# A two-group encoder layer in split precision: two sets of plane buffers in branch b, the factor of x moved into the gates, other PSUM banks for two sums

## The chip, the cores and the metric

The kernel runs on one core of a Trainium2 chip. The metric is the device time of one launch in microseconds (us). Three runs of the kernel before gave 1679.86, 1680.59 and 1681.42; their median is 1680.59 us.

## The reference, cut to what matters

One layer of an encoder, computed for two request groups (256 prompt frames and 64 sample frames, 320 columns together) that share all weights. D is 2048.

```python
xn = rmsnorm(x, norm_mix)
proj = xn @ w_in                       # q k v u vs: 1024 columns each; g: 4096
q, k, v, u, vs, g = split(proj)
a = stick_breaking(q, k, v)            # the sample group also sees cached k, v
bb = spatial_gate(gelu(u), rmsnorm(gelu(vs), sgu_norm))
g_a, g_b = split(sigmoid(g + b_gate))
merged = g_a * (a @ w_branch_a) + g_b * (bb @ w_branch_b)
h = x + merged @ w_out
hn = rmsnorm(h, norm_ffn)
gu = hn @ w_gate_up
h = h + (silu(gu[..., :D_FF]) * gu[..., D_FF:]) @ w_down
return rmsnorm(h, norm_final), k, v, vs
```

`rmsnorm` is x times a factor for each frame (`rx` in the kernel) times a gain for each channel. `x @ w` times `rx` is the same as `(x * rx) @ w`, so the kernel may put `rx` on either side of a projection.

## The kernel before, in words

All matrices are worked in blocks of 128 rows; D has 16 of them (`KD`). Activations lie transposed, channels on the partitions and the 320 frames along the row. To keep float32 accuracy with the fast multiply, each operand is split into a high part and the low rest, and three products are summed: high x high, high weight x low activation, low weight x high activation.

Weights come from HBM by the queue of the sync engine (SP), 512 KB a load, into three buffers `raw` (a fourth, `raw2`, serves every fourth load while the pool of the spatial gate is open: `state["more"]`). The scalar engine (ACT) rounds a load to its high part `wh` (L296, or L105 for plain blocks), the vector engine (DVE) subtracts to get the low part (`wl` or `low`, L297, L106).

Two shapes of work use them. A plain **block** (L135) sums three products for one output block in one `acc` bank of PSUM. A **quad** (L310) makes four output blocks at once. Its high half swaps the operands: 80 matmuls of 128x512 (L328) with pieces of the activation as the moving weights of the array fill three main banks, which hold four output blocks with frames on the partitions. When the next quad or block begins, `flush` runs `finish`: 64 low matmuls of 128x320 (L335) into four more banks, each copied out at once by ACT (L357) or DVE (L359). The main banks are copied as two 16-bit planes into `flat` (the first by ACT, L379, right behind the high half; the second behind the copy of the second low sum, by ACT, L387, or DVE, L389), each plane is transposed by a DMA from SP (L380, L390) into `turned`, the two planes are joined back into `flat` (L397 on ACT, L399 on DVE) and added to the low sums (L405, L406). `flat` and `turned` are one buffer each in the pool `wide`. PSUM has a ring of three `acc` banks, a ring of four `aux` and a single `aux1`. In branch b and in the gates successive quads take their main banks from `acc` and `aux` in turn; elsewhere always from `acc`.

The order of the work: the first projections; then the list `PLAN` (k3 as two plain blocks, quads of k, q, v, then q2 and v2 as blocks, quads for vs and u) with pieces of attention and spatial gate put between; branch a as 16 plain blocks of `w_a`; branch b as four quads of `w_b` with eight k-blocks (40 + 32 matmuls); eight gate quads (g0 to g7, two for each group of four output blocks, `i` = 0 for branch a's gate and 1 for branch b's); the output projection, the feed-forward part, the last norm. A counter of ticks, one for each weight load consumed, sets when a join, an add or a step of the spatial gate is issued (`at`, with `LAG`, `LB`, `LG`, `SGU`). Each engine works through its instructions in the order they were issued.

During branch a, x is scaled by `rx` and split anew (`rescale` to `rewide`, L824 to L841), so that the gates come out scaled. Before that, every projection of x is multiplied by `rx` afterwards (L423 `times_rx`, L693 for blocks).

Names for the prediction: L288 is the weight load of a quad, L508 and L510 scans of the attention, L693 the copy of a plain block, L821 the copy of a block of branch a, L869 a gate's sigmoid, L884 its product with the branch, L873 and L876 the split of the merged rows, L939 a load of x by the GpSimd engine (POOL) for the output projection.

Of the kernel before, what the change touches and what calls it, by code (L numbers as in the profile page):

```python
# [9 lines left out]
F32 = mybir.dt.float32  # L10
F32R = mybir.dt.float32r
U16 = mybir.dt.uint16
AF = mybir.ActivationFunctionType
ALU = mybir.AluOpType

P = 128
TP = 256
TS = 64
# [11 lines left out]
NEG = -1.0e30  # L30
QSCALE = 128.0 ** -0.5
WARM = 8
LAG = {'h': 6, 's': 7, 'u': 9, 'b': 6}
BQ = [0, 4]
MR = 1
GL = 1
# [7 lines left out]
LU = (5, 0)  # L44
LD = (6, 5, 0)
LO = (10, 6)
LG = (10, 8)
LB = 9
PF = {'h': 1, 's': 0, 'u': 0, 'b': 0, 'g': 1, 'o': 1, 'f': 1}
JN = {'h': 1, 's': 1, 'u': 0, 'b': 1, 'g': 0, 'o': 0, 'f': 0}  # L50
ATD = (1, 3, 1, 1, 4, 3, 3)
SGU = (3, 2, 1, 6)
MIX = (3, 4)
SC = (7, 1)
PLAN = (('N', 'k3'), ('Q', 'k1', 'q1'), ('Q', 'v1', 'k2'), ('N', 'q2', 'v2'), ('Q', 'q3', 'v3'), ('Q', 's0', 's1'), ('Q', 's2', 's3'), ('Q', 'u0', 'u1'), ('Q', 'u2', 'u3'))
PL = {'h': 0, 's': 0, 'u': 1, 'g': 1, 'o': 1, 'f': 1, 'b': 1}
ST = {'h': 1, 's': 1, 'u': 0, 'g': 0, 'o': 0, 'f': 1, 'b': 1}
LW = {'h': 1, 's': 1, 'u': 1, 'g': 0, 'o': 1, 'f': 0, 'b': 0}


@with_exitstack
def stream_step(ctx: ExitStack, tc: tile.TileContext, xT, w_in, w_a, w_b, w_out, w_gu, w_down,
# [69 lines left out]
        nc.tensor.matmul(ps[:, :T], a, x[1], start=False, stop=False)  # L132
        nc.tensor.matmul(ps[:, :T], b, x[0], start=False, stop=last)  # L133

    def block(src, act, banks=None):  # L135
        flush()
        ps = (banks or acc)()
        nk = len(act)
        for k0 in range(0, nk, HALF):
            n = min(HALF, nk - k0)  # L140
            w = weights(src[:, k0 * P : (k0 + n) * P], n)
            for j in range(n):
                product(ps, w, j, act[k0 + j], k0 + j == 0, k0 + j == nk - 1)
            tick()
        return ps[:, :T]

# [127 lines left out]
        nc.vector.tensor_copy(t, got["rx"][:, 0:1])  # L274

    count = [0, 0]
    wide = {}

    def flush():
        if state["pending"]:  # L280
# [29 lines left out]
    def quad(src, xs, parts, done, lag=10, alternate=True, nk=KD, addend=None, cut=None, step=None):  # L310
        lows = []
        stage = state["stage"]
        qpool = wide["pool"]
        ready_ = [split(src, c) for c in range(0, 2 * PF[stage], 2)] if state["pending"] else []
        flush()
        banks, others = (acc, aux) if count[1] % 2 == 0 or not alternate else (aux, acc)
        main = [banks() for _ in range(3)]
        count[1] += 1

        def high(c):  # L320
            wh, wl = ready_.pop(0) if ready_ else split(src, c)
            wh = wh.rearrange("p (b k) -> p b k", b=4)
            lows.append(wl)
            for j in range(2):
                k = c + j
                w = wh[:, :, j * P : (j + 1) * P]
                for i, x in enumerate(pieces(xs[k])):
                    nc.tensor.matmul(main[i // 2].rearrange("p (b m) -> p b m", b=4), x, w,  # L328
                                     start=k == 0 and i % 2 == 0, stop=k == nk - 1 and (i % 2 == 1 or i == 4))
            tick()  # L330

        def low(ps, b, k0, k1):
            for k in range(k0, k1):
                at0 = (2 * b + k % 2) * P
                nc.tensor.matmul(ps[:, :T], lows[k // 2][:, at0 : at0 + P], highs(xs[k]), start=k == 0, stop=k == nk - 1)  # L335

        held = []
        if cut:
            for c in range(0, cut, 2):
                high(c)  # L340
            for b in range(4):
                held.append((others, others, others, aux1)[b]())
                low(held[b], b, 0, cut)
                tick()
        for c in range(cut or 0, nk, 2):
            high(c)
        sums = parts()
        turning = first_plane(main)

        def finish():  # L350
            now = state["tick"]
            for b in range(4):
                ps = held[b] if cut else ((others, others, aux1, aux) if alternate else (aux, aux1, aux, aux1))[b]()
                low(ps, b, cut or 0, nk)
                to = next(t[:, b - b0, :] for t, b0, nb in sums if b0 <= b < b0 + nb)
                if addend is None and LW[stage]:
                    copied = nc.scalar.copy(out=to, in_=ps[:, :T])  # L357
                elif addend is None:
                    copied = nc.vector.tensor_copy(to, ps[:, :T])  # L359
                else:  # L360
                    copied = nc.vector.tensor_tensor(out=to, in0=ps[:, :T], in1=addend[:, b, :], op=ALU.add)
                if b == 1:
                    with tc.issue_after(copied.ins):
                        second_plane(stage, main, *turning)
                tick()
            joined(stage, now + lag, ST[stage] if step is None else step, copied.ins, sums, *turning, done)

        state["pending"] = finish
        return sums
# [2 lines left out]
        return main[c].bitcast(U16).rearrange("p (n w) -> p n w", w=2)[:, :, 1 - i]  # L372

    def first_plane(main):
        flat = wide["pool"].tile([P, 12 * P], F32, tag="flat", name="flat")
        turned = wide["pool"].tile([P, 2, 12, P], U16, tag="turned", name="turned")
        plane = flat.bitcast(U16)[:, 0 : 12 * P]
        for c in range(3):
            tc.keep_in_program_order(nc.scalar.copy(out=plane[:, c * 512 : (c + 1) * 512], in_=half_words(main, c, 0)))  # L379
        nc.sync.dma_start_transpose(out=turned[:, 0], in_=plane)  # L380
        return flat, turned
# [416 lines left out]
    for mode, *names in PLAN:  # L798
        state["stage"] = {"s": "s", "u": "u"}.get(names[0][0], "h")
        if mode == "N":  # L800
            for name in names:
                t = place(name)
                for j in range(2):
                    one_block(name, j, t, block(columns(name)[j], narrow))
        else:
            a, b = names
            src = tuple(columns(n) for n in names)
            if a[0] == b[0] and int(b[1]) == int(a[1]) + 1:
                b0 = "qkvus".index(a[0]) * H + 2 * int(a[1])
                src = w_in[b0 : b0 + 4]  # L810
            quad(src, wide_xs,
                 lambda names=names: [(place(n), 2 * i, 2) for i, n in enumerate(names)],
                 lambda i, names=names: pair_done(names[i]), LAG[state["stage"]], False)
# [1 line left out]
    state["stage"] = "g"  # L815

    def projected(i, m, src, act):
        ps = block(src[m], act)
        if m % 2 == 0:
            branch[i].append(pair("ab"[i]))  # L820
        nc.scalar.copy(out=branch[i][m // 2][:, m % 2, :], in_=ps)  # L821

    def rescale(m):
        both = xs[m][2]  # L824
        hi, lo = both[:, 0:T], both[:, T + TS : WIDE]
        t = t320("ev")
        with tc.issue_after(state["split"].ins):
            nc.vector.tensor_tensor(out=t, in0=hi.bitcast(F32), in1=lo.bitcast(F32), op=ALU.add)
            nc.vector.tensor_tensor(out=t, in0=t, in1=got["rx"], op=ALU.mult)
        at(state["tick"] + 1, resplit, both, t)  # L830

    def resplit(both, t):
        nc.scalar.copy(out=both[:, 0:T], in_=t)
        at(state["tick"] + 1, relow, both, t)

    def relow(both, t):
        nc.vector.tensor_tensor(out=both[:, T + TS : WIDE], in0=t, in1=both[:, 0:T].bitcast(F32), op=ALU.subtract)
        at(state["tick"] + 1, rewide, both)

    def rewide(both):  # L840
        nc.scalar.copy(out=both[:, T : T + TS], in_=both[:, WIDE - TS : WIDE].bitcast(F32))  # L841

    for m in range(KD):
        at(state["tick"] + SC[0] + SC[1] * m, rescale, m)
    def branched(i, src, act):
        for q in range(KD // 4):
            if q >= BQ[i]:
# [11 lines left out]
    flush()  # L859
    count[0] += C0  # L860
    count[1] = P0
    branched(1, w_b, bT)

    state["more"] = None
    mix_ctx.close()
    merged = []

    def gate(t, i, m):
# [10 lines left out]

    def gate_done(tiles, i, q, h, of):  # L880
        t = tiles[h][0]
        for j in range(2):
            gate((t[:, j, :], t[:, j, :]), i, 4 * q + 2 * h + j)
        nc.vector.tensor_tensor(out=t, in0=t, in1=branch[i][2 * q + h], op=ALU.mult)  # L884
        if i:
            a = of[h][0]
            nc.vector.tensor_tensor(out=t, in0=a, in1=t, op=ALU.add)
            for j in range(2):
                merge(t[:, j, :], 4 * q + 2 * h + j)

    last = KD // 4 - 1
    for q in range(KD // 4):
        of = []
        for i in range(2):
# [4 lines left out]
            def parts(tiles=tiles):  # L899
                tiles.extend((pair("g"), b, 2) for b in (0, 2))  # L900
                return tiles

            m = 5 * H + i * KD + 4 * q
            quad(w_in[m : m + 4], wide_xs, parts, lambda h, a=(tiles, i, q), of=of: gate_done(*a, h, of),
                 LG[q == last])
# [3 lines left out]
    for j in range(0 if GL else 4):  # L909
        m = 4 * last + j  # L910
        ps = block(w_in[5 * H + KD + m], narrow)
        t = t320("ev")
        gate((t, ps), 1, m)
        nc.vector.tensor_tensor(out=t, in0=t, in1=branch[1][m // 2][:, m % 2, :], op=ALU.mult)
        nc.vector.tensor_tensor(out=t, in0=of[j // 2][0][:, j % 2, :], in1=t, op=ALU.add)
        merge(t, m)
# [376 lines left out]
```

## Time and profile before

| | us |
|---|---|
| median of three runs | 1680.59 |
| the profiled execution | 1680.71 |
| its span | 1678.8 |
| TensorE busy | 1664.2 |
| VectorE busy | 1097.9 |
| ScalarE busy | 853.3 |
| mean granted clock of TensorE | 0.996 |

Times inside the trace count from the start of its span. TensorE is PE, its weight load PEld; "idle before, releaser" says how long an engine stood before an instruction and what ended it. A matmul of 512 columns starts 0.227 us after the one before it at full clock, one of 320 columns 0.147 us. The stretches that the change touches:

| stretch | starts at, us |
|---|---|
| first quad of `PLAN` | 65.84 |
| branch a, 16 blocks | 308 |
| branch b, 4 quads | 364.47 |
| first gate quad g0 | 419.60 |
| second gate quad | 454.24 |
| third gate quad | 481.78 |
| output projection | about 647 |

### The profile page before, as it was taken

How to read it: one execution, taken by the hardware profiler on the slowest of the kernel's cores; microseconds unless marked ns; L12 is line 12 of the kernel's file. 1: busy time of each engine (PE TensorE's matmuls, PEld its weight loads, DVE VectorE, ACT ScalarE, POOL GpSimd, SP SyncE). 2: the span in 40 equal slices, each digit the busy share in tenths (PEclk: the TensorE clock that was granted, in tenths of full speed). 3: DMA queues.
4: the chain of work that ended last, by engine and by line, in shares of the span. 5: the costliest groups of instructions: out<-in, count | busy, mean ns of one | idle time of the engine just before them, and what ended most of it. 6: DMA issues, size and time to landing. Idle time of an engine off the chain costs nothing.

```text
span 1678.8 us, 23399 instructions
## 1 busy us (share of the span) xinstructions
PE 1664.2 (99%) x9032; PEld 1492.4 (89%) x9032; DVE 1097.9 (65%) x1510; ACT 853.3 (51%) x1252; POOL 67.0 (4%) x77
## 2 busy tenths in 40 slices
PE   9999999999899999999999999999999999999998
PEld 9889888998788888888989898989898888888897
DVE  7566678865566675677565656565656565566776
ACT  7555677554554544565544444344445443435464
POOL 1100002000000000000000000000000000000000
PEclk9999999999999999999999999999999999999999
DMA  7669679557757665767565666665665666665663
GB/s 265 192 168 240 193 175 244 167 167 168 194 176 201 183 183 176 207 186 196 163 197 161 206 161 202 164 201 166 192 175 183 179 179 188 178 185 175 186 177 115
DMA packets 433711, 311.30 MB, mean 185 GB/s; under 512 B 201632, under 2 KB 422816, under 8 KB 433600
## 3 DMA queue, kind: packets, MB, share of 16 engines
q1 hardware_dynamic: 430000, 300.99, 63.8%
q0 software_dynamic: 2368, 8.26, 1.6%
q8 instruction: 70, 1.15, 0.3%
q10 hardware_dynamic: 1232, 0.57, 0.1%
q14 instruction: 41, 0.34, 0.1%
HBM read 256.03 MB, written 5.51 MB: 156 GB/s over the span
## 4 chain that ended last, share of the span: by engine, by line
PE 94%; DMA 2%; ACT 2%; SPq 1%; DVE 1%; issue 0%; ACTq 0%; DVEq 0%
PE acc L328 30%; PE aux L328 24%; PE aux L335 22%; PE acc L335 6%; PE acc L131 2%; PE acc L132 2%; PE acc L133 2%; DMA turned<-flat 1%; PE aux L1012 1%; PE aux L133 1%; PE aux L131 1%; PE aux L132 1%; ACT wh L296 1%; DMA raw<-w_in 1%; PE acc L1012 0%
## 5 line engine op out<-in xcount | busy, mean ns | idle before, releaser
L296 ACT CAST wh<-raw 128x1024 fp32r<-128x1024 f32 x420 | 442.6, 1057 | 655.8 <-DMA raw<-w_gu 258.5
L328 PE MATMUL acc<-wh,A 128*128 128x512 f32 x1760 | 405.3, 390 | 0.7 <-DVE k L693 0.7
L328 PEld LDWEIGHTS acc<-wh,A 128*128 128x128 f32 x1760 | 328.9, 188 | 69.1 <-DVE k L693 1.1
L297 DVE TENSOR_TENSOR low<-raw,wh 128x1024 fp32r<-128x1024 f32 x233 | 281.2, 1219 | 117.1 <-ACT wh L296 109.6
L297 DVE TENSOR_TENSOR wl<-raw,wh 128x1024 fp32r<-128x1024 f32 x187 | 226.6, 1220 | 91.8 <-ACT wh L296 87.8
L328 PE MATMUL aux<-wh,A 128*128 128x512 f32 x1200 | 277.1, 391 | 4.4 <-DVE b L359 4.3
L328 PEld LDWEIGHTS aux<-wh,A 128*128 128x128 f32 x1200 | 225.9, 189 | 51.5 <-DVE b L359 4.7
L335 PE MATMUL aux<-A,low 128*128 128x320 f32 x1020 | 171.3, 309 | 0.0
L335 PEld LDWEIGHTS aux<-A,low 128*128 128x128 f32 x1020 | 155.4, 188 | 1.4 <-issue 0.4
L335 PE MATMUL aux<-A,wl 128*128 128x320 f32 x868 | 147.7, 309 | 0.4 <-ACT k L357 0.4
L359 DVE COPY sum<-aux 128x320 f32<-128x320 f32 x91 | 44.4, 488 | 140.5 <-PE aux L335 140.4
L335 PEld LDWEIGHTS aux<-A,wl 128*128 128x128 f32 x868 | 132.7, 188 | 1.4 <-ACT k L357 0.7
L399 DVE COPY flat<-turned 128x1536 uint16<-128x1536 uint16 x101 | 104.4, 1051 | 20.0 <-DMA turned<-flat 20.0
L328 PE MATMUL aux<-wh,act 128*128 128x512 f32 x368 | 86.2, 389 | 0.0
L328 PE MATMUL acc<-wh,act 128*128 128x512 f32 x368 | 86.1, 389 | 0.0
L328 PEld LDWEIGHTS acc<-wh,act 128*128 128x128 f32 x368 | 68.9, 188 | 14.1
L328 PEld LDWEIGHTS aux<-wh,act 128*128 128x128 f32 x368 | 68.8, 188 | 14.0
L105 ACT CAST wh<-raw 128x1024 fp32r<-128x1024 f32 (+2 forms) x48 | 45.9, 959 | 31.6 <-issue 9.5
L106 DVE TENSOR_TENSOR wl<-raw,wh 128x1024 fp32r<-128x1024 f32 (+2 forms) x48 | 53.2, 1111 | 12.5 <-ACT wh L105 10.9
L963 POOL TENSOR_TENSOR sum<-sum,rh 128x640 f32<-128x640 f32 x18 | 28.0, 1581 | 664.4 <-ACT sum L962 664.4
L379 ACT COPY flat<-acc 128x512 uint16<-128x512 uint16 x93 | 48.2, 586 | 2.9 <-DVE b L406 1.7
L359 DVE COPY sum<-acc 128x320 f32<-128x320 f32 x29 | 14.2, 490 | 49.2 <-PE acc L335 49.0
(301 smaller groups left out, 2193.2 us busy)
## 6 DMA issues: line engine op xcount, KB each, us to landing
raw<-w_gu SPq DMA_DIRECT2D x176, 512.0 KB, 4.2
raw<-w_in SPq DMA_DIRECT2D x117, 512.0 KB, 4.5
raw<-w_down SPq DMA_DIRECT2D x84, 512.0 KB, 4.3
raw<-w_out SPq DMA_DIRECT2D x32, 512.0 KB, 4.6
raw<-w_in SPq DMA_DIRECT2D x53, 256.0 KB, 3.8
raw<-w_a SPq DMA_DIRECT2D x16, 512.0 KB, 4.3
raw<-w_b SPq DMA_DIRECT2D x16, 512.0 KB, 3.5
sum<-xT POOLq DMA_DIRECT2D x4, 640.0 KB, 6.8
```

The lines of the kernel that those rows point to most:

```text
L105: cast = nc.scalar.copy(out=wh[:, : n * P], in_=raw[:, : n * P])
L106: state["split"] = nc.vector.tensor_tensor(out=wl[:, : n * P], in0=raw[:, : n * P], in1=wh[:, : n * P].bitcast(F32), op=ALU.subtract)
L131: nc.tensor.matmul(ps[:, :T], a, x[0], start=first, stop=False)
L132: nc.tensor.matmul(ps[:, :T], a, x[1], start=False, stop=False)
L133: nc.tensor.matmul(ps[:, :T], b, x[0], start=False, stop=last)
L296: cast = nc.scalar.copy(out=wh, in_=raw)
L297: state["split"] = nc.vector.tensor_tensor(out=wl, in0=raw, in1=wh.bitcast(F32), op=ALU.subtract)
L328: nc.tensor.matmul(main[i // 2].rearrange("p (b m) -> p b m", b=4), x, w, start=k == 0 and i % 2 == 0, stop=k == nk - 1 and (i % 2 == 1 or ...
L335: nc.tensor.matmul(ps[:, :T], lows[k // 2][:, at0 : at0 + P], highs(xs[k]), start=k == 0, stop=k == nk - 1)
L359: copied = nc.vector.tensor_copy(to, ps[:, :T])
L379: tc.keep_in_program_order(nc.scalar.copy(out=plane[:, c * 512 : (c + 1) * 512], in_=half_words(main, c, 0)))
L399: nc.vector.tensor_copy(to, of)
```

## The change

It has three parts. First, branch b's four quads use two sets of `flat` and `turned` in turn: one in `wide`, one in a new pool `turns`, which takes the place of the spatial gate's pool. That pool, and with it the fourth weight buffer, is therefore given up before branch b and not after it; `turns` is closed before the third gate quad. In branch b both joins move to DVE (`JN`), the first weight load of a quad is split ahead of the low half of the quad before (`PF`), and joins come two ticks later (`LAG`). Second, `rescale` and what follows it are gone; the gates are multiplied by `rx` when they are done. Third, the fourth low sum of a quad with fixed banks goes to `aux` where it went to `aux1`, and the last plain block of each `N` entry of `PLAN` to `aux` where it went to `acc`; a plain block is now copied out before the tick that ends it. Besides, steps of the spatial gate move by a tick or two, the last gate quad's joins come two ticks later, and the second plane of the u quads goes from ACT to DVE (`PL`).

```diff
-LAG = {'h': 6, 's': 7, 'u': 9, 'b': 6}
+LAG = {'h': 6, 's': 7, 'u': 9, 'b': 8}
-LG = (10, 8)
+LG = (10, 10)
-PF = {'h': 1, 's': 0, 'u': 0, 'b': 0, 'g': 1, 'o': 1, 'f': 1}
-JN = {'h': 1, 's': 1, 'u': 0, 'b': 1, 'g': 0, 'o': 0, 'f': 0}
+PF = {'h': 1, 's': 0, 'u': 0, 'b': 1, 'g': 1, 'o': 1, 'f': 1}
+JN = {'h': 1, 's': 1, 'u': 0, 'b': 0, 'g': 0, 'o': 0, 'f': 0}
-SGU = (3, 2, 1, 6)
+SGU = (4, 1, 1, 5)
-PL = {'h': 0, 's': 0, 'u': 1, 'g': 1, 'o': 1, 'f': 1, 'b': 1}
+PL = {'h': 0, 's': 0, 'u': 0, 'g': 1, 'o': 1, 'f': 1, 'b': 1}
-    def block(src, act, banks=None):
+    def block(src, act, banks=None, then=None):
...
+            if then and k0 + n == nk:
+                then(ps[:, :T])
             tick()
...
-                ps = held[b] if cut else ((others, others, aux1, aux) if alternate else (aux, aux1, aux, aux1))[b]()
+                ps = held[b] if cut else ((others, others, aux1, aux) if alternate else (aux, aux1, aux, aux))[b]()
...
     def first_plane(main):
-        flat = wide["pool"].tile([P, 12 * P], F32, tag="flat", name="flat")
-        turned = wide["pool"].tile([P, 2, 12, P], U16, tag="turned", name="turned")
+        of = wide["other"].pop() if wide["other"] else wide["pool"]
+        flat = of.tile([P, 12 * P], F32, tag="flat", name="flat")
+        turned = of.tile([P, 2, 12, P], U16, tag="turned", name="turned")
...
-                    one_block(name, j, t, block(columns(name)[j], narrow))
+                    block(columns(name)[j], narrow, aux if j and name == names[-1] else None, lambda ps: one_block(name, j, t, ps))
...
-    def rescale(m):
...
-            nc.vector.tensor_tensor(out=t, in0=hi.bitcast(F32), in1=lo.bitcast(F32), op=ALU.add)
-            nc.vector.tensor_tensor(out=t, in0=t, in1=got["rx"], op=ALU.mult)
...
-    for m in range(KD):
-        at(state["tick"] + SC[0] + SC[1] * m, rescale, m)
...
-    branched(1, w_b, bT)
-
     state["more"] = None
     mix_ctx.close()
+    turn_ctx = ExitStack()
+    turns_b = turn_ctx.enter_context(tc.tile_pool(name="turns", bufs=1))
+    wide["other"] = [turns_b, wide["pool"]] * (KD // 8)
+    branched(1, w_b, bT)
...
     def gate_done(tiles, i, q, h, of):
         t = tiles[h][0]
+        times_rx(t)
...
+            if q == 1 and not i:
+                turn_ctx.close()
```

Line numbers of the changed kernel are 2 to 3 higher than before up to L821, and then 13 lower: L297, L359, L380, L390, L399, L405, L406 are L299, L361, L383, L393, L402, L408, L409.

The first place is DVE around the second quad of branch b. Before:

```order
L297 TENSOR_TENSOR low<-raw_4083,wh 128x1024
L359 COPY b<-aux_4010 128x320
L359 COPY b<-aux 128x320
L399 COPY flat<-turned 128x1536
L405 TENSOR_TENSOR b<-flat,b 128x640 x2
L406 TENSOR_TENSOR b<-flat,b 128x2x64 x2
L297 TENSOR_TENSOR low<-raw,wh 128x1024 x3
L359 COPY b<-acc 128x320 x2
```

And now (the copies at the end free the banks of the quad after it):

```order
L361 COPY b<-aux_3922 128x320
L361 COPY b<-aux 128x320
L402 COPY flat<-turned 128x1536
L299 TENSOR_TENSOR low<-raw,wh 128x1024
L402 COPY flat<-turned 128x1536
L408 TENSOR_TENSOR b<-flat,b 128x640 x2
L409 TENSOR_TENSOR b<-flat,b 128x2x64 x2
L299 TENSOR_TENSOR low<-raw,wh 128x1024 x2
L361 COPY b<-acc 128x320 x2
```

The other join has come over from ACT, and one subtraction stands between the two joins. The second place is SP in branch b. Before:

```order
L288 DMA raw<-w_b 128x4x256 x3
L380 DMA_TRANSPOSE turned<-flat 128x12x128
L390 DMA_TRANSPOSE turned<-flat 128x12x128
L288 DMA raw_4083<-w_b 128x4x256
L288 DMA raw<-w_b 128x4x256 x3
L380 DMA_TRANSPOSE turned<-flat 128x12x128
L390 DMA_TRANSPOSE turned<-flat 128x12x128
L288 DMA raw_4208<-w_b 128x4x256
L288 DMA raw<-w_in 128x4x256 x3
L380 DMA_TRANSPOSE turned<-flat 128x12x128
```

And now (`raw_4083` and `raw_4208` were loads into the fourth buffer):

```order
L290 DMA raw<-w_b 128x4x256 x10
L383 DMA_TRANSPOSE turned<-flat 128x12x128
L393 DMA_TRANSPOSE turned<-flat 128x12x128
L290 DMA raw<-w_b 128x4x256 x3
L383 DMA_TRANSPOSE turned<-flat 128x12x128
L393 DMA_TRANSPOSE turned<-flat 128x12x128
L290 DMA raw<-w_b 128x4x256 x3
L290 DMA raw<-w_in 128x4x256
L383 DMA_TRANSPOSE turned<-flat 128x12x128
```

Three or four loads still stand between two pairs of transposes, all now into the three buffers, and ten loads of `w_b` are ahead of the first pair. The third place is PE at the end of k3's second block and in the first quad. Before:

```order
L133 MATMUL acc<-A,wl 128x320
L328 MATMUL acc<-wh,A 128x512 x80
...
L335 MATMUL aux<-A,low 128x320 x8
L335 MATMUL aux_1042<-A,wl 128x320 x8
L335 MATMUL aux_1042<-A,low 128x320 x8
```

And now (`aux_1042` was the second use of the single bank `aux1`):

```order
L133 MATMUL aux<-A,wl 128x320
L330 MATMUL acc<-wh,A 128x512 x80
...
L337 MATMUL aux<-A,low 128x320 x8
L337 MATMUL aux<-A,wl 128x320 x8
L337 MATMUL aux<-A,low 128x320 x8
```

The block has left the ring from which the quad takes its three main banks, and the fourth low sum has left the single bank.

More of the change, by code (lines that the diff above doesn't have):

```diff
@@ L46 @@
 LO = (10, 6)
-LG = (10, 8)
+LG = (10, 10)
 LB = 9
-PF = {'h': 1, 's': 0, 'u': 0, 'b': 0, 'g': 1, 'o': 1, 'f': 1}
-JN = {'h': 1, 's': 1, 'u': 0, 'b': 1, 'g': 0, 'o': 0, 'f': 0}
+PF = {'h': 1, 's': 0, 'u': 0, 'b': 1, 'g': 1, 'o': 1, 'f': 1}
+JN = {'h': 1, 's': 1, 'u': 0, 'b': 0, 'g': 0, 'o': 0, 'f': 0}
 ATD = (1, 3, 1, 1, 4, 3, 3)
-SGU = (3, 2, 1, 6)
+SGU = (4, 1, 1, 5)
 MIX = (3, 4)
-SC = (7, 1)
+SC = (5, 1)
 PLAN = (('N', 'k3'), ('Q', 'k1', 'q1'), ('Q', 'v1', 'k2'), ('N', 'q2', 'v2'), ('Q', 'q3', 'v3'), ('Q', 's0', 's1'), ('Q', 's2', 's3'), ('Q', 'u0', 'u1'), ('Q', 'u2', 'u3'))
-PL = {'h': 0, 's': 0, 'u': 1, 'g': 1, 'o': 1, 'f': 1, 'b': 1}
+PL = {'h': 0, 's': 0, 'u': 0, 'g': 1, 'o': 1, 'f': 1, 'b': 1}
 ST = {'h': 1, 's': 1, 'u': 0, 'g': 0, 'o': 0, 'f': 1, 'b': 1}
-LW = {'h': 1, 's': 1, 'u': 1, 'g': 0, 'o': 1, 'f': 0, 'b': 0}
+LW = {'h': 1, 's': 1, 'u': 1, 'g': 0, 'o': 0, 'f': 0, 'b': 0}
 @with_exitstack
@@ L276, in stream_step @@
     count = [0, 0]
-    wide = {}
+    wide = {"other": []}
     def flush():
@@ L817, in projected @@
     def projected(i, m, src, act):
-        ps = block(src[m], act)
         if m % 2 == 0:
             branch[i].append(pair("ab"[i]))
-        nc.scalar.copy(out=branch[i][m // 2][:, m % 2, :], in_=ps)
-    def rescale(m):
[L824 to L827, printed above, removed]
-            nc.vector.tensor_tensor(out=t, in0=hi.bitcast(F32), in1=lo.bitcast(F32), op=ALU.add)
[L829 to L841, printed above, removed]
-    for m in range(KD):
-        at(state["tick"] + SC[0] + SC[1] * m, rescale, m)
+        to = branch[i][m // 2][:, m % 2, :]
+        block(src[m], act, None, lambda ps: nc.scalar.copy(out=to, in_=ps))
     def branched(i, src, act):
@@ L912, in stream_step @@
         t = t320("ev")
-        gate((t, ps), 1, m)
+        nc.vector.tensor_tensor(out=t, in0=ps, in1=got["rx"], op=ALU.mult)
+        gate((t, t), 1, m)
         nc.vector.tensor_tensor(out=t, in0=t, in1=branch[1][m // 2][:, m % 2, :], op=ALU.mult)
```

## The prediction

> **What bounds the kernel now.** I read the page's table of engines first, then the list of what TensorE (PE) waited for, then the windows of branch b.
>
> ```profile
> span 1678.8 us, 23399 instructions
> ...
> PE 1664.2 (99%) x9032; PEld 1492.4 (89%) x9032; DVE 1097.9 (65%) x1510; ACT 853.3 (51%) x1252; POOL 67.0 (4%) x77
> ```
> ```profile
> PE aux L328 <- DVE b L359: 4.3, 1, 4.3
> ...
> PE acc L328 <- DVE k L693: 0.7, 1, 0.7
> ...
> PE aux L335 <- ACT k L357: 0.4, 1, 0.4
> ```
>
> PE is busy 99% of the span, and the change issues the same matmuls in the same order (only bank names differ). What it can gain is therefore PE's idle time and the time PE runs at a lower clock; what it can lose is any new wait of PE. Three waits are in places that the change edits: 4.3 us at the end of branch b, 0.7 us and 0.4 us in the first quad.
>
> The windows show the last quad of branch b, the first 10.4 us of gate quad g0 in two pieces, and the two gate quads behind g0; columns are us, PE, PEld, DVE, ACT, POOL busy with counts, granted clock, DMA share, GB/s.
>
> ```profile
> 405.82:419.60 13.78, 13.77 (x73) 11.84 (x72) 4.51 (x8) 3.87 (x5) 0.54 (x1) 1.00 0.82 196
> 419.60:425.00 5.40, 1.15 (x5) 0.47 (x4) 5.37 (x9) 3.69 (x6) 0.00 (x0) 0.76 0.39 123
> 425.00:430.00 5.00, 4.89 (x13) 3.88 (x14) 2.47 (x5) 2.59 (x5) 0.00 (x0) 0.58 1.05 245
> ...
> 454.24:481.78 27.54, 27.54 (x146) 24.40 (x145) 16.50 (x21) 14.32 (x19) 0.00 (x0) 1.00 0.64 182
> 481.78:509.32 27.54, 27.54 (x146) 24.40 (x145) 19.66 (x32) 14.48 (x22) 0.54 (x1) 1.00 0.57 177
> ```
>
> A quad of branch b takes 13.78 us (so the branch starts four of them before 419.60, at 364.48) and a whole gate quad 27.54. But g0 takes from 419.60 to 454.24, 34.64 us. **The loss at this seam is 7.1 us**: 4.3 of the wait, about 2.1 more because the clock stood at 0.58 after it (5.00 x 0.42), and 0.7 of small gaps. Why PE waited, the chain of waits shows:
>
> ```profile
> 403.26 1.58 ACT flat L379 x3
> ...
> 406.31 0.96 ACT wh L296
> ...
> 410.12 6.95 DMA turned<-flat
> 417.17 1.96 ACT flat L397
> 419.16 0.84 DVE b L405
> 420.23 1.22 DVE wl L297
> ...
> 423.52 1.14 DVE wl L297
> 424.65 0.41 DVE b L359
> 425.11 19.91 PE aux L328 x78
> ```
>
> One `flat` serves all quads, so a quad's first plane (L379) waits until the quad before is joined and added; PE's third matmul of g0 needs a bank that DVE copies (L359) behind those adds in its queue. The loop runs on into g0.
>
> **The b seam after the change.** With two sets, a first plane no longer waits for the quad before. What stays is DVE's order, from the rows shown in the section on the change: first join, one subtraction, second join, adds, then a subtraction that frees the `raw` buffer of a weight load which stands ahead of the next transposes on SP. So landing, DVE, load and transposes still form a loop. Its terms:
>
> ```profile
> 374.68 2.18 SPq L380 DMA_TRANSPOSE turned<-flat  x1
> ...
> 390.56 3.76 SPq L380 DMA_TRANSPOSE turned<-flat  x1
> ...
> 397.00 0.53 SPq L288 DMA_DIRECT2D raw<-w_b  x1
> ...
> 406.50 3.57 SPq L380 DMA_TRANSPOSE turned<-flat  x1
> ```
> ```profile
> 382.56 1.05 DVE L399 COPY flat<-turned 128x1536 uint16<-128x1536 uint16 x1 [3.44 <-DMA turned<-flat]
> ...
> 398.62 1.10 DVE L399 COPY flat<-turned 128x1536 uint16<-128x1536 uint16 x1 [5.39 <-DMA turned<-flat]
> 400.62 1.56 DVE L405 TENSOR_TENSOR b<-flat,b 128x640 f32<-128x640 f32 x2 [0.90 <-ACT flat L397]
> ...
> 402.51 3.49 DVE L297 TENSOR_TENSOR low<-raw,wh 128x1024 fp32r<-128x1024 f32 x3
> ...
> 417.19 1.07 DVE L399 COPY flat<-turned 128x1536 uint16<-128x1536 uint16 x1 [7.88 <-DMA turned<-flat]
> ```
>
> From the first transpose's issue to the join are 7.88, 8.06 and 10.69 us. The third is the odd one: its transposes were in flight with a 640 KB load of x.
>
> ```profile
> 409.19 0.54 POOL L939 DMA_DIRECT2D sum<-xT  x1 [130.13 <-DMA raw<-w_in]
> ```
>
> That load now waits for the buffers of the second set, so it leaves this place. I take 8.0 for a landing. The DVE part is one join 0.95 (starts lie a tenth closer than durations), a subtraction 1.14 (three in 3.49), a join 0.95, the adds 1.89 (400.62 to 402.51) and a subtraction 1.14: 6.07, with the load's issue 0.53 together 6.6 us. Counting from 364.48, the first transposes land at 18.1 as now (382.56). The second are issued at 24.7 and land at 32.7; the third are issued at 39.3 and land at 47.3. Behind that stand on DVE two joins with a subtraction between, the adds, two subtractions and the copy that PE needs (0.41): 7.6 us, so at 54.9. PE starts g0 at 55.1 and needs the bank with its third matmul, 2 x 0.227 later, at 55.6. **It comes 0.7 us early; the landings of the second and third pair may average 8.3 before PE waits.** That is thin, and it is the point on which the forecast hangs. Gain of the seam: 7.1 us, ends 0 and 7.1, and below 0 if the landings grow past those of now.
>
> Branch b also has three `raw` buffers where it had four. A b quad takes four loads in 13.78 us, 3.4 each; a buffer is held for the landing (3.5 in the row below), a cast (0.96 in the chain) and a subtraction (1.14), 5.6 in all, so three give one in 1.9. No cost, unless DVE stands at a join, which is the loop above.
>
> ```profile
> raw<-w_b SPq DMA_DIRECT2D x16, 512.0 KB, 3.5
> ```
>
> A stall can cost more than its length, by the clock. Here the window after the 4.3 us wait shows 0.58; the 0.7 us wait of the first quad is followed by one matmul 0.1 us late only. The Trainium skill, "TensorE: Matmul & The Clock Gate", The HAM clock gate, says that the clock halves after an idle window of about 3.4 us, and that this window runs freely. The trace agrees with it on both sides of that figure. As an estimate from that page of the Trainium skill, a wait of 2 us that stayed at the seam would cost no more than itself, while the same share of clock loss as now (2.1 for 4.3) would make it 3.
>
> **The first quad.**
>
> ```profile
> 65.84 0.63 PE L328 MATMUL acc<-wh,A 128*128 128x512 f32 x2
> ...
> 66.62 0.48 DVE L693 TENSOR_TENSOR k<-acc,rx 128x320 f32<-128x320 f32 x1
> ...
> 67.16 2.11 PE L328 MATMUL acc<-wh,A 128*128 128x512 f32 x8 [0.69 <-DVE k L693]
> ```
> ```profile
> 90.32 1.19 PE L335 MATMUL aux<-A,low 128*128 128x320 f32 x7
> ...
> 91.08 0.77 ACT L357 COPY k<-aux 128x320 f32<-128x320 f32 x2
> ...
> 91.91 0.85 PE L335 MATMUL aux<-A,wl 128*128 128x320 f32 x4 [0.40 <-ACT k L357]
> ```
>
> The quad's third matmul was due at 65.84 + 0.45 = 66.29 and came at 67.16: 0.87, with a slow one behind 0.97. It needs the bank of the plain block before it. That block now sits in an `aux` bank, and the third `acc` bank held a block that was emptied one block earlier: all of 0.97 goes. The fourth low sum was due at 90.32 + 7 x 0.147 = 91.35 and came at 91.91: 0.56, with the next 0.66. It shared the single `aux1` bank with the second sum, copied just before; an `aux` bank is a ring of four: 0.66 goes. Next late would be the attention's use of the ring, whose copies this trace shows no PE wait for. Ends 0 and 1.6; I take 1.6, since the rows name the releaser.
>
> **What is taken out and put in elsewhere.**
>
> ```profile
> L829 DVE TENSOR_TENSOR ev<-ev,rx 128x320 f32<-128x320 f32 x16 | 7.8, 485 | 0.1
> ...
> 308.00:364.47 56.47, 56.47 (x392) 56.47 (x391) 48.51 (x87) 32.30 (x68) 0.00 (x0) 1.00 0.45 153
> ```
>
> The rescale of x goes: 16 x 3 such DVE rows, 23.3 us, and 32 ACT casts. PE is busy 56.47 of 56.47 us there, so nothing is gained. The gates get 16 products of 128x640, two a quad; the adds of the same form are 1.56 for two, so DVE has 18.1 and 21.2 us of 27.54. Place on the path:
>
> ```profile
> 502.96 1.98 DVE L876 TENSOR_TENSOR m<-g,m 128x64 fp32r<-128x64 f32 x8 [1.30 <-ACT m L873]
> 504.92 0.88 DVE L359 COPY g<-acc 128x320 f32<-128x320 f32 x2
> ```
>
> The copy that frees the next quad's bank is done at 505.3 and due at 509.32 + 0.45, 4.4 us early; with 1.56 more ahead of it 2.9 us early. Cost 0; without that cover 8 x 1.56 = 12.5. The u quads' second plane goes from ACT to DVE, two quads of three copies, and the ticks of the spatial gate and of the last gate quad shift; PE's list has no wait in either stretch, so 0, with ends of -0.5 and +0.5 (the nearest waits are the 0.4 and 0.7 above).
>
> **Sum.** 7.1 + 0.97 + 0.66 = 8.7; I leave 0.2 for the small gaps at the start of g0, whose releaser no row names. 1680.71 for the profiled execution less 8.5 is **1672.2 us**. The profiled execution lies 0.12 above the median of 1680.59, so the forecast serves for both.
>
> **Rivals.**
> *Part of the wait comes back at the seam.* For it: the margin is 0.7 us, landings reached 10.7 once, and two landings enter the loop, so a late microsecond in each counts twice. Against: the x load is gone from there, and both landings without it took 8. At a mean of 9.3 PE waits 2 x 1.3 - 0.7 = 1.9 us: 1674.1. At 10.2 it waits 3.7 us, 1675.9, and with half of the clock loss of now 1677.0.
>
> *The two sets change nothing at the seam.* If both landings take 10.7 the third ends 5.4 us later and PE waits 4.7 with the clock loss behind it: only the 1.6 of the first quad stays, 1679.1. For it: DVE's order, not `flat`, is then the loop. Against: 7.88 and 8.06 without the x load.
>
> *Slower: the gates' products lie on the path.* If the copies of the gate quads have no slack, each of eight quads grows by 1.56: 1672.2 + 12.5 = 1684.7. It decides when the 2.9 us of slack are used up, by landings about 3 us later in every gate quad. Against: DVE idles 6 to 9 us of each quad.
>
> **How the numbers follow.** Forecast 0.58 (1671.3 to 1673.5), part of the wait 0.27 (1673.5 to 1677.3), nothing at the seam 0.10, slower 0.05. The range 1671.3 to 1677.3 holds the first two, 0.85. About 0.2% (3.4 us) is what a measurement of this kernel can tell from no change: below 1677.2 counts as faster, 0.85; within 0.10; slower 0.05.
>
> **What would show it.** In the list of PE's waits the rows of L693 and of the 0.4 us are gone, and that of `b` (then L361) gone or under 4 us. The windows of g0 show clock 1.00 from its start, and g0 takes about 27.7 us. The first plane's copies in branch b lie 13.8 us apart, the joins wait for transposes that landed 8 us after issue, and the x load comes behind g0. The gate quads stay at 27.54. The forecast is wrong if the landings exceed 8.3 in the mean, if a gate quad is longer, or if PE waits in the out projection, where the last merged block now comes later.

## The result, and the profile after

The changed kernel takes 1671.55 us (median of six runs, 1671.29 to 1672.06) against 1680.22 for the kernel before in the same measurement. The ratio is 0.9948, with a 95% interval of 0.9935 to 0.9961: 8.7 us less, where 8.4 to 8.5 were forecast. One launch of an experiment (old order, below) took 7731.9 us and is left out of its ratio. The first fences have rows of the page and of the list of PE's waits.

```profile
span 1670.3 us, 23317 instructions
...
PE 1660.4 (99%) x9032; PEld 1490.8 (89%) x9032; DVE 1097.5 (66%) x1488; ACT 836.3 (50%) x1210; POOL 67.0 (4%) x77
```
```profile
PE aux L212 <- POOL eps_t L171: 1.0, 1, 1.0
PE acc L1146 <- ACT sq L981: 0.5, 1, 0.5
...
PE acc L330 <- ACT wh L298: 0.2, 1, 0.2
```

The three waits shown before are gone. PE's busy time fell by 3.8 us with the same matmuls; the low clock behind the wait at g0, 2.1 us, is part of that. The last row is new: in the first quad PE, now earlier, waits at 79.17 for a cast (L298); by starts it loses 0.5 us there. Two more rows of 0.3 us, at 4.84 and 17.71, come and go among the kernels below. The windows show g0, and further on a gate quad of branch b's gate:

```profile
418.52:446.06 27.54, 27.54 (x145) 24.41 (x145) 13.79 (x18) 11.35 (x14) 0.54 (x1) 1.00 0.77 208
...
473.60:501.14 27.54, 27.54 (x145) 24.40 (x145) 21.14 (x34) 13.56 (x21) 0.54 (x1) 1.00 0.62 181
```

g0 takes 27.54 us at full clock where it took 34.64: all 7.1 us of the seam came back. The gate quads stayed at 27.54 with DVE at 21.1. Now SP, DVE and ACT in branch b, each from the timeline:

```profile
373.43 2.26 SPq L383 DMA_TRANSPOSE turned<-flat  x1
375.75 1.67 SPq L393 DMA_TRANSPOSE turned<-flat  x1
377.51 9.32 SPq L290 DMA_DIRECT2D raw<-w_b  x3
387.31 2.23 SPq L383 DMA_TRANSPOSE turned<-flat  x1
...
400.99 2.19 SPq L383 DMA_TRANSPOSE turned<-flat  x1
```
```profile
380.16 1.06 DVE L402 COPY flat<-turned 128x1536 uint16<-128x1536 uint16 x1 [2.29 <-DMA turned<-flat]
...
393.79 1.05 DVE L402 COPY flat<-turned 128x1536 uint16<-128x1536 uint16 x1 [2.08 <-DMA turned<-flat]
...
408.58 1.04 DVE L402 COPY flat<-turned 128x1536 uint16<-128x1536 uint16 x1 [3.15 <-DMA turned<-flat]
...
413.20 0.49 DVE L409 TENSOR_TENSOR b<-flat,b 128x128 f32<-128x128 f32 x2
...
415.88 0.88 DVE L361 COPY b<-aux 128x320 f32<-128x320 f32 x2
```
```profile
385.68 1.56 ACT L382 COPY flat<-acc 128x512 uint16<-128x512 uint16 x3 [0.59 <-PE acc L330]
...
399.40 1.56 ACT L382 COPY flat<-aux 128x512 uint16<-128x512 uint16 x3 [0.53 <-PE aux L330]
...
413.19 1.56 ACT L382 COPY flat<-acc 128x512 uint16<-128x512 uint16 x3 [0.53 <-PE acc L330]
```

The first-plane copies (L382) wait for PE alone and lie 13.7 to 13.8 us apart. From the first transpose's issue to the join are 6.73, 6.48 and 7.59 us. The first copy that g0 needs ends at 416.4 and is due at 418.35 + 0.45, so it comes 2.4 us early, not 0.7. One thing doesn't fit the story of the two sets: the adds of the third quad end at 413.7 and the fourth quad's first plane starts at 413.19, so a shared buffer could have cost only half a microsecond here.

### The profile page after: what moved, and what is told of

Its sections match the earlier page's. It is cut to its first block, busy times and chain, and to the rows that moved or that the text cites. A ratio compares the mean times of both kernels' runs of the same rounds, so it can differ in the third digit from the quotient of the medians.

```text
span 1670.3 us, 23317 instructions
## 1 busy us (share of the span) xinstructions
PE 1660.4 (99%) x9032; PEld 1490.8 (89%) x9032; DVE 1097.5 (66%) x1488; ACT 836.3 (50%) x1210; POOL 67.0 (4%) x77
## 4 chain that ended last, share of the span: by engine, by line
PE 98%; DMA 1%; DVE 0%; SPq 0%; ACT 0%; issue 0%; DVEq 0%; ACTq 0%
PE acc L330 32%; PE aux L330 25%; PE aux L337 23%; PE acc L337 7%; PE acc L133 2%; PE acc L131 2%; PE acc L132 2%; PE aux L131 1%; PE aux L132 1%; PE aux L999 1%; PE aux L133 1%; DMA x<-xT 0%; PE acc L999 0%; DMA raw<-w_in 0%; PE aux L1016 0%; PE acc L1016 0%
## 5 line engine op out<-in xcount | busy, mean ns | idle before, releaser
L298 ACT CAST wh<-raw 128x1024 fp32r<-128x1024 f32 x420 | 443.5, 1057 | 680.2 <-DMA raw<-w_gu 272.4
L299 DVE TENSOR_TENSOR low<-raw,wh 128x1024 fp32r<-128x1024 f32 x233 | 281.6, 1219 | 118.5 <-ACT wh L298 112.5
L299 DVE TENSOR_TENSOR wl<-raw,wh 128x1024 fp32r<-128x1024 f32 x187 | 226.6, 1219 | 82.9 <-ACT wh L298 82.5
L361 DVE COPY sum<-aux 128x320 f32<-128x320 f32 x91 | 44.4, 488 | 139.8 <-PE aux L337 139.7
L402 DVE COPY flat<-turned 128x1536 uint16<-128x1536 uint16 x105 | 108.4, 1050 | 11.2 <-DMA turned<-flat 11.2
L382 ACT COPY flat<-acc 128x512 uint16<-128x512 uint16 x93 | 48.1, 586 | 3.3 <-PE acc L330 3.2
L361 DVE COPY sum<-acc 128x320 f32<-128x320 f32 x29 | 14.2, 490 | 51.2 <-PE acc L337 51.0
```

The source lines that it names most:

```text
L298: cast = nc.scalar.copy(out=wh, in_=raw)
L299: state["split"] = nc.vector.tensor_tensor(out=wl, in0=raw, in1=wh.bitcast(F32), op=ALU.subtract)
L402: nc.vector.tensor_copy(to, of)
```

## The experiments

Each ratio is to the kernel before on the same chip, with its 95% interval; the chips gave 1680.22 to 1681.21 for that kernel, so medians of different chips compare to about 1 us. "Wait at g0" is PE's wait for L361 (L359) in the profile.

| kernel | median us | ratio | wait at g0, us |
|---|---|---|---|
| the change | 1671.55 | 0.9948 (0.9935 to 0.9961) | none |
| one set | 1671.66 | 0.9944 (0.9928 to 0.9961) | none |
| x scaled in branch a | 1671.56 | 0.9947 (0.9932 to 0.9962) | none |
| order only | 1673.72 | 0.9958 (0.9944 to 0.9973) | none |
| old ticks | 1673.76 | 0.9966 (0.9953 to 0.9979) | 1.7 |
| old split | 1674.33 | 0.9963 (0.9950 to 0.9975) | 3.2 |
| old join | 1677.04 | 0.9974 (0.9963 to 0.9985) | 3.0 |
| old order | 1677.19 | 0.9974 (0.9962 to 0.9985) | 2.7 |
| three raw buffers only | 1677.90 | 0.9986 (0.9976 to 0.9995) | 2.0 |
| x load moved only | 1678.12 | 0.9987 (0.9977 to 0.9996) | 1.6 |
| two sets only | 1678.85 | 0.9990 (0.9981 to 1.0000) | 3.0 |
| banks only | 1679.26 | 0.9992 (0.9982 to 1.0001) | 4.3 |
| extra x loads | 1679.76 | 1.0000 (0.9990 to 1.0009) | 2.4 and others |

**One set.** The changed kernel with one buffer in branch b.

```diff
-    wide["other"] = [turns_b, wide["pool"]] * (KD // 8)
+    wide["other"] = []
```

> The changed kernel, but branch b keeps one flat/turned buffer for all four quads. Theory S (the shared buffer made the loop, the second set broke it): the first plane copies of branch b wait for the adds again, PE waits some 4 us at the start of g0 and loses 2 more by the clock: about 1678.5 us. Rival L (the transposes now land 6.5 to 7.6 us after issue, in place of 7.9 to 10.7, and that broke the loop): the adds end at 384.8+0.5, 398.9 and 413.7 in the changed kernel's trace, before or 0.5 us behind the next first plane copy at 385.7, 399.4 and 413.2, so one buffer is enough and the time stays at 1671.5 to 1672.

Rival L holds. The one first plane that waited for the adds is this; ACT stood 0.85 us where it stands 0.53 to 0.58 for PE ahead of the other three, so it came some 0.3 us late, and no PE wait follows:

```profile
412.79 1.56 ACT L382 COPY flat<-acc 128x512 uint16<-128x512 uint16 x3 [0.85 <-DVE b L409]
```

The second set is worth nothing beside the new order.

**Old order.** The changed kernel with branch b's three numbers as before.

```diff
-LAG = {'h': 6, 's': 7, 'u': 9, 'b': 8}
+LAG = {'h': 6, 's': 7, 'u': 9, 'b': 6}
-PF = {'h': 1, 's': 0, 'u': 0, 'b': 1, 'g': 1, 'o': 1, 'f': 1}
+PF = {'h': 1, 's': 0, 'u': 0, 'b': 0, 'g': 1, 'o': 1, 'f': 1}
-JN = {'h': 1, 's': 1, 'u': 0, 'b': 0, 'g': 0, 'o': 0, 'f': 0}
+JN = {'h': 1, 's': 1, 'u': 0, 'b': 1, 'g': 0, 'o': 0, 'f': 0}
```

> The changed kernel with the numbers of before for branch b: first join on ACT, no split ahead of the low half, joins two ticks earlier (JN 1, PF 0, LAG 6). Two sets and three raw buffers stay. Theory S: the order matters little, 1671.5 to 1673. Rival O (the new order on DVE did it): ACT stands at its join, the casts behind it come late and the wait at g0 returns, 1675 or more.

Two sets don't help without the new order: 2.7 us of wait are back and 5.6 us of time. Rival O holds.

**Two sets only, and banks only**, each in the kernel before.

```diff
...
-    branched(1, w_b, bT)
-
     state["more"] = None
     mix_ctx.close()
+    turn_ctx = ExitStack()
+    turns_b = turn_ctx.enter_context(tc.tile_pool(name="turns", bufs=1))
+    wide["other"] = [turns_b, wide["pool"]] * (KD // 8)
+    branched(1, w_b, bT)
...
```

> The kernel before with two flat/turned sets in branch b and, for their room, three raw buffers there; every other part as before. Theory S: the loss at the seam goes, 7.1 us, about 1673.2. Rival O: the loss stays for the most part, 1678 or more.

```diff
...
-                ps = held[b] if cut else ((others, others, aux1, aux) if alternate else (aux, aux1, aux, aux1))[b]()
+                ps = held[b] if cut else ((others, others, aux1, aux) if alternate else (aux, aux1, aux, aux))[b]()
...
-                    one_block(name, j, t, block(columns(name)[j], narrow))
+                    block(columns(name)[j], narrow, aux if j and name == names[-1] else None, lambda ps: one_block(name, j, t, ps))
```

> The kernel before with the two other PSUM banks alone (fourth low sum in aux, last plain block of an N entry in aux and copied before the tick). The waits of 0.7 us (L693) and 0.4 us go, worth 0.97 + 0.66 = 1.6 us by the sum; the changed kernel's trace shows a new wait of 0.5 us for a cast at 79.2, so 1.1 is left: about 1679.1. If the new wait came from another part, 1678.6.

Two sets alone leave 3.0 of the 4.3 us, so rival O holds here too. Nor is the rest due to them. The kernel with three raw buffers only, below, has one set and is otherwise close to this one: three buffers for weights, and no x load in branch b (444.04 here). It is no slower, at 1677.90 with 2.0 us of wait. The banks alone give 1.7 us by the medians (1680.92 for the kernel before on that chip; the interval of the ratio takes in 1), and their list of waits lacks both rows of the first quad:

```profile
PE aux L330 <- DVE b L361: 4.3, 1, 4.3
PE aux L212 <- POOL eps_t L171: 1.0, 1, 1.0
PE acc L1161 <- ACT sq L996: 0.5, 1, 0.5
```

The new cast wait at 79 us isn't among them either; nor is it in the trace of one set. It comes and goes from one execution to the next.

**The x load, and the buffers.** In the kernel before, the x load held back until the first merged row; and the kernel before with the fourth weight buffer given up ahead of branch b.

```diff
-        if q == 0:
+        if q <= 1:
             nc.vector.tensor_copy(x[:, 0, 0:1], merged[0][:, 0:1].bitcast(F32))
```

> The kernel before, but the 640 KB load of x that ran at 409.19 waits (as the one behind it does) for the first merged row, so that it leaves branch b. If that load made the third landing 10.7 us, the landing falls to about 8, the adds of the third quad end 2.7 us earlier, PE's wait at g0 falls from 4.3 to about 1.6 and the clock loss goes: 1680.2 - 2.7 - 2 = about 1675.5. If the landing was long for another reason, 1680.

```diff
+    state["more"] = None
     branched(1, w_b, bT)
-    state["more"] = None
```

> The kernel before with the fourth weight buffer given up before branch b (state more set to None ahead of it), one flat/turned set, the old order. If fewer weight loads in flight shorten the landings (6.5 to 7.6 us in the changed kernel, 7.9 to 10.7 before), they fall by about 1.3 us each, the loop of three gives 3 to 4 us and PE's wait at g0 falls to 1 or less: 1675 to 1676. If the buffers don't matter: 1680, or slower by what the loads now wait for.

Without the x load the third landing fell from 10.69 to 7.65 us (issue 406.31, join 413.96), and the wait from 4.3 to 1.6. The kernel with the banks only, whose x load runs at 407.31, repeats the long landing (10.63), so the load does lengthen it. But not every long landing is its work: two sets only and the old order, which have no x load there, show 9.15 and 9.54 for the third pair. The time fell by 2.2 us only (3.1 in the profiled execution), less than the 4.7 expected; a new wait of 1.6 us for a cast stands behind it in g0 (at 432.38). Three buffers left the first two landings as they were (8.05 and 8.17). The third fell to 8.09, but the x load is gone from branch b in this kernel too (352.75), so its 2.4 us look like the same gain, and nothing is left that the buffers would have to explain.

```profile
390.33 3.89 SPq L380 DMA_TRANSPOSE turned<-flat  x1
...
406.31 3.44 SPq L380 DMA_TRANSPOSE turned<-flat  x1
...
413.96 1.07 DVE L399 COPY flat<-turned 128x1536 uint16<-128x1536 uint16 x1 [4.83 <-DMA turned<-flat]
```

**x scaled in branch a.** The changed kernel with `rescale` put back and without the product in the gates.

```diff
-SC = (5, 1)
+SC = (7, 1)
...
     def gate_done(tiles, i, q, h, of):
         t = tiles[h][0]
-        times_rx(t)
...
+    for m in range(KD):
+        at(state["tick"] + SC[0] + SC[1] * m, rescale, m)
...
```

> The changed kernel with x scaled and split anew during branch a again, and the gates without the product by rx. By the prediction both sides are hidden by PE: 1671.5 plus or minus 0.4. If the 23 us of DVE and 11 us of ACT work beside branch a, or the 13 us of DVE work in the gates, stood on the path, it would be off by over 1 us.

1671.56: both ways are hidden.

**Extra x loads.** The changed kernel with a load beside each pair of transposes.

```diff
+        if wide.get("turn"):
+            seen = wide["turn"].tile([P, 2, T], F32, tag="seen", name="seen")
+            nc.scalar.copy(out=seen[:, 0, 0:1], in_=flat[:, 0:1])
+            nc.gpsimd.dma_start(out=seen, in_=xT[:, 0:2, :])
...
```

> The changed kernel with an extra load of 320 KB of x by POOL's queue started right ahead of the first transposes of each of the first quads of branch b (its data isn't used). In the kernel before, 640 KB went with a landing 2.7 us longer. If contention scales, each landing grows by about 1.3 us, the third pair's adds end some 3.5 us later than now, and of the 2.0 us by which the copy for g0 is early (416.8 against 418.8) nothing is left: PE waits about 1.5 us, 1673. If contention of such a load isn't what made that landing long: 1671.6.

The landings grew by more than expected, to 10.68, 8.70 and 9.84 us. PE then waited twice in branch b too, at 391.2 and 406.8, 5.3 us in all with the wait at g0, by starts; the profiled execution is the shortest of this kernel, whose median is 8.2 us above the changed kernel's. Longer landings are not all of it: the second pair is also issued 3.2 us after its plane is ready (387.03 and 390.24), and a weight load slips between its two transposes (392.63). The margin of the change is real, and small.

**Which of the three numbers.** First all three in the kernel before, with one set, four raw buffers, the x load in its place, the old banks and x scaled in branch a; then each put back by itself in the changed kernel (old join, old split, old ticks).

```diff
-LAG = {'h': 6, 's': 7, 'u': 9, 'b': 6}
+LAG = {'h': 6, 's': 7, 'u': 9, 'b': 8}
-PF = {'h': 1, 's': 0, 'u': 0, 'b': 0, 'g': 1, 'o': 1, 'f': 1}
+PF = {'h': 1, 's': 0, 'u': 0, 'b': 1, 'g': 1, 'o': 1, 'f': 1}
-JN = {'h': 1, 's': 1, 'u': 0, 'b': 1, 'g': 0, 'o': 0, 'f': 0}
+JN = {'h': 1, 's': 1, 'u': 0, 'b': 0, 'g': 0, 'o': 0, 'f': 0}
```

> The kernel before with the three numbers of branch b alone (JN 0, PF 1, LAG 8): one flat/turned set, four raw buffers, the x load at its place, old banks, rescale kept. Theory Q (what counts is that one weight load fewer stands ahead of the second pair of transposes on SP, three in place of four, so that they are issued when the plane is ready and don't share the DMA engines with that load): most of the 7.1 us go, the x load may give back up to 2: 1673 to 1675. Theory R (three raw buffers are needed too): 1676 to 1679.

By its ratio the order alone takes 7.1 us (4.5 to 9.4 by the interval), as much as the seam's loss, and the time is in theory Q's range. In its trace g0 takes 27.54 us (419.45 to 446.99). Its list of waits has no row for b, while that of L693 in the first quad is still there:

```profile
PE acc L328 <- DVE k L693: 0.7, 1, 0.7
```

This with the x load in the middle of the branch (407.05): the third landing is 9.07 us there, and PE doesn't wait. But the copy for g0 ends at 419.60 and is due at 419.45 + 0.45, only 0.3 us early. Here the one `flat` does hold two first planes back, by about 1 us, and PE doesn't notice:

```profile
387.72 1.56 ACT L379 COPY flat<-acc 128x512 uint16<-128x512 uint16 x3 [1.53 <-DVE b L406]
...
417.08 1.56 ACT L379 COPY flat<-acc 128x512 uint16<-128x512 uint16 x3 [1.74 <-DVE b L406]
```
```profile
419.11 0.89 DVE L359 COPY b<-aux 128x320 f32<-128x320 f32 x2
```

```diff
-JN = {'h': 1, 's': 1, 'u': 0, 'b': 0, 'g': 0, 'o': 0, 'f': 0}
+JN = {'h': 1, 's': 1, 'u': 0, 'b': 1, 'g': 0, 'o': 0, 'f': 0}
```

> The changed kernel with the first join of branch b on ACT again (JN 1). Still three loads ahead of the second pair of transposes, but a load now stands between the two transposes of a pair. Theory Q: 1671.5 to 1673. Rival A (ACT standing at its join, with the casts behind it, made the loss): 1675 or more, with PE waiting at the start of g0.

```diff
-PF = {'h': 1, 's': 0, 'u': 0, 'b': 1, 'g': 1, 'o': 1, 'f': 1}
+PF = {'h': 1, 's': 0, 'u': 0, 'b': 0, 'g': 1, 'o': 1, 'f': 1}
```

> The changed kernel without the split ahead of the low half in branch b (PF 0). Four loads stand ahead of the second pair of transposes again. Theory Q: the pair is issued some 0.9 us after the plane is ready and lands in over 8 us, PE waits 1 to 3 us at the start of g0, 1673 to 1677. Rival A: 1671.5 to 1672.

```diff
-LAG = {'h': 6, 's': 7, 'u': 9, 'b': 8}
+LAG = {'h': 6, 's': 7, 'u': 9, 'b': 6}
```

> The changed kernel with the joins of branch b two ticks earlier (LAG 6). Four loads stand ahead of the second pair of transposes, and joins and adds stand ahead of the subtractions on DVE. Theory Q: as without the early split, 1673 to 1677. Rival A: 1671.5 to 1672.

Each of the three is needed: each put back brings a wait at g0 back, of 3.0, 3.2 and 1.7 us, and the old join and the old split make PE wait in branch b as well (1.4 us at 406.48, 0.7 us at 405.69). Old split and old ticks come out in theory Q's range and not at rival A's 1671.5 to 1672. Theory Q names the right place for two of them, the second pair of transposes on SP. With the old split:

```profile
377.57 11.86 SPq L290 DMA_DIRECT2D raw<-w_b  x4
389.64 4.08 SPq L383 DMA_TRANSPOSE turned<-flat  x1
393.77 2.51 SPq L393 DMA_TRANSPOSE turned<-flat  x1
```
```profile
398.00 2.00 DVE L402 COPY flat<-turned 128x1536 uint16<-128x1536 uint16 x2 [4.49 <-DMA turned<-flat]
```

Its plane is ready at 387.00 (385.44 + 1.56), but four loads stand ahead, the last of which waits for its buffer; the first transpose is issued 2.6 us late and takes 4.08 us of SP where it takes 2.23 in the changed kernel. The same reading over the kernels:

| kernel | loads ahead of the second pair, between the two | plane ready to first join, us |
|---|---|---|
| the change | 3, 0 | 387.24 to 393.79: 6.55 |
| one set | 3, 0 | 386.51 to 392.94: 6.43 |
| order only | 3, 0 | 389.28 to 395.89: 6.61 |
| x scaled in branch a | 3, 0 | 386.90 to 394.50: 7.60 |
| old join | 3, 1 | 387.53 to 396.85: 9.32 |
| old order | 4, 0 | 387.33 to 396.45: 9.12 |
| old ticks | 4, 0 | 386.76 to 396.61: 9.85 |
| x load moved only | 4, 0 | 388.52 to 398.46: 9.94 |
| the kernel before | 4, 0 | 388.76 to 398.62: 9.86 |
| banks, two sets, three raw buffers only | 4, 0 | 9.77, 9.96, 9.95 |
| old split | 4, 0 | 387.00 to 398.00: 11.00 |
| extra x loads | 3, 1 | 387.03 to 398.94: 11.91 |

Three loads and none between give 6.4 to 7.6 us; a fourth load, ahead or between, 9.1 to 11.0, and 11.9 with the extra x loads. What tells seems to be the waiting, rather than the count. With x scaled in branch a the third load too is issued late, and the pair 1.4 us behind its plane, hence the 7.60. And ahead of the third pair the changed kernel has four loads as well, but the last of them goes at 400.08, before the plane is ready at 400.96: from there to the join are 7.62 us. For the old join, theory Q expected 1673 at most and missed: it overlooked the load between, and behind it the join on ACT holds the casts, as rival A says. How the 3.0 us of this kernel divide between the two was not taken apart. Nor was the fourth load moved by itself: that it is the cause is read from SP's queue and from the table, and the three numbers are what was shown.

## Why the prediction was right, and where it was not

*The total.* 1672.2 was forecast and 1671.55 measured. The windows hold the 7.1 of the seam, and branch b starts 1.24 us earlier (363.23 in place of 364.47), where 1.63 were summed for the first quad.

*The seam's mechanism.* This is the step that failed, though its sum held. The prediction said that one `flat` makes a first plane wait, and that "With two sets, a first plane no longer waits for the quad before". One set does as well (1671.66), and two sets without the order do not (1677.19 and 1678.85). In the timeline of the kernel before, neither the second nor the third first plane waited for the adds:

```profile
387.22 1.54 ACT L379 COPY flat<-acc 128x512 uint16<-128x512 uint16 x3
...
398.61 1.99 ACT L397 COPY flat<-turned 128x1536 uint16<-128x1536 uint16 x1 [7.43 <-DMA turned<-flat]
400.42 2.98 ACT L296 CAST wh<-raw 128x1024 fp32r<-128x1024 f32 x3
403.26 1.58 ACT L379 COPY flat<-aux 128x512 uint16<-128x512 uint16 x3
...
423.63 1.56 ACT L379 COPY flat<-acc 128x512 uint16<-128x512 uint16 x3 [1.71 <-DVE b L406]
```
```profile
378.67 11.79 SPq L288 DMA_DIRECT2D raw<-w_b  x4
```

The second was ready at 388.76, and its transpose was issued at 390.56, behind four loads. That lateness carried on: the third stood on ACT behind the join of that pair and three casts, without a gap. Only the fourth waited for the adds, and the copy that ended PE's wait at g0 stands on DVE behind the join of the third pair, not behind that plane. The prediction read the rows of the chain at 403 as a wait for the buffer; ACT's order and the load ahead of the transposes made them late.

Why did the number hold? The sum kept a loop over DVE and a load ahead of the transposes, and that loop is longer than what the changed kernel shows: its second and third pairs are issued 0.07 and 0.03 us after their planes are ready (387.24 and 400.96), and the planes wait for PE. Whatever is done before PE needs the bank gives the same 7.1. That the order, which does the work, came in one change with the buffers, to which the gain was put down, is luck.

*The landing.* 8.0 us was taken and 6.5 to 7.6 came, so the margin was 2.4 us and not 0.7. Landings scatter, though. With x scaled in branch a, and the same order in branch b, they are 8.30, 6.20 and 7.79 us and the margin is 1.7; with the order alone it is 0.3. That it can be used up is what the extra x loads show.

*The x load.* It left the place, as said (431.88 in the changed kernel), and it did make the third landing long (10.69 against 7.65 without it). But the gain doesn't hang on it: with the new order the wait is gone with the load still there, with 0.3 us to spare.

*The first quad.* 0.97 goes in every trace of the new banks. The 0.66 was no steady loss: of the five traces with the old banks the kernel before alone shows it, the kernel with the x load moved loses about 0.35 us there, and the three others none. And 0.4 to 0.5 comes back as late matmuls behind a cast, in two of the nine traces with the new banks (the change and the old order).

*Rescale and the gates.* Nothing, as forecast: 1671.56 with both undone. The slower rival fell with it.

*The clock.* By the prediction's estimate from the Trainium skill, "TensorE: Matmul & The Clock Gate", The HAM clock gate, a wait of 2 us would have cost no more than itself. That fell: after 2.0 us of wait the granted clock was 0.65 (three raw buffers only, below).

## What to carry to other kernels

Where a DMA is late, look first at what its queue issues ahead of it and what that waits for; a late issue looks like a slow landing, and like a missing buffer, to whoever sums from the waiter's side. Before a second buffer is paid for, compare in the trace the end of the last reader with the start of the next writer, and then ask whether anybody waits for that writer: in the changed kernel they overlapped by half a microsecond at most, and with the order alone the writer was held back by 1 us at no cost. When a change has several parts, the one that gives it its name may be the one that does nothing, and three numbers in a table the ones that do most of it.

## What the runs showed of the hardware

The low clock follows a wait at g0 without a fixed length. The windows behind the wait of three kernels, columns as before:

```profile
422.14:427.00 4.86, 4.86 (x14) 3.85 (x15) 2.36 (x4) 2.48 (x5) 0.00 (x0) 0.65 0.97 233
```
```profile
423.00:428.00 5.00, 5.00 (x15) 3.99 (x16) 3.22 (x5) 1.04 (x1) 0.00 (x0) 0.66 1.11 254
```
```profile
423.50:428.50 5.00, 5.00 (x22) 4.11 (x23) 2.28 (x4) 0.00 (x0) 0.00 (x0) 1.00 1.04 242
```

Three raw buffers only, after 2.0 us of wait: clock 0.65. Old split, after 3.2 us: 0.66. Old join, after 3.0 us: 1.00. Of the others, two sets only (3.0 us) and the old order (2.7) show 0.66 and 0.69 in such a window, extra x loads (2.4), old ticks (1.7) and x load moved only (1.6) show 1.00. So a wait of 2 us can cost 1.7 us more (4.86 x 0.35) and one of 3 us none. The kernels with such a wait also scatter more: old split took from 1672.56 to 1678.57 us, the changed kernel from 1671.29 to 1672.06. That the clock makes this scatter is likely but wasn't shown, since one execution of each was traced.

How much a transfer beside a pair of transposes costs isn't settled: 640 KB of x went with a landing 3.0 us longer, 320 KB with 2.2 to 4.0. Each is one landing of one execution, and landings without any x load beside them run from 6.2 (x scaled in branch a) to 9.5 us (old order), and to 10.4 with a weight load between the two transposes (old join).
